# A two-layer decoder trunk: the MLPs' wide products in two halves of the tokens

## The chip, the cores and the metric

The kernel runs on one core of one Trainium2 chip. The metric is the device time of one execution in microseconds (us), shown as the median of several runs. The engines are TensorE (PE, matmuls; its weight loads are listed apart as PEld), VectorE (DVE), ScalarE (ACT), GpSimd (POOL) and SyncE (SP, which issues most DMAs). Each has its own queue of instructions, and they wait for one another by semaphores.

## The reference

Two layers, 512 tokens, 1024 features. Each layer is a mixer (layer 0: sliding-window attention beside a short convolution; layer 1: gated linear attention), an MLP, and a gated embedding of the layer. The MLP, cut to what matters here:

```python
D_MODEL, SEQ, D_FF = 1024, 512, 2816

def _conv_ffn(h, w_up, conv_w, conv_b, w_down):
    u = _causal_depthwise_conv(h @ w_up, conv_w) + conv_b      # width 3, over the tokens
    gate, up = jnp.split(u, 2, axis=-1)
    return (jax.nn.gelu(gate, approximate=False) * up) @ w_down

# in each layer i
x = x + mixer(rms_norm(x, mix_norm[i]))
x = x + _conv_ffn(_rms_norm(x, ffn_norm[i]), ffn_w_up[i], ffn_conv_w[i], ffn_conv_b[i], ffn_w_down[i])
x = x + _per_layer_embedding(x, p[i], ple_norm[i], ple_w_gate[i], ple_w_proj[i])
```

## The kernel before

*Numbers.* All is float32. An operand is split into a high part in the type that PE reads in one pass (float32r) and the rest, the low part; a product is then three matmuls, high by high, high by low and low by high (`mm3`, L162, lines 166 to 168). ACT makes the high part with a copy, DVE the low part with a subtraction: `split` (L100) for activations, `cut` (L129) for weights. The transposed activations `xT[m]` hold 128 features by 512 tokens; the operands of the MLP are `xg[k]`, eight pairs of 128 x 512. In a matmul here a block of 128 x 128 weights is loaded, and the tokens move past it: 512 columns in a plain product.

*Up-projection (`ffn`, L906).* A layer's 5632 columns are done in 11 groups of 256 gate columns and 256 value columns. The gate columns of a group go through a block scheme with seven products instead of eight (`seven`, L860): four weight blocks, two halves of the tokens, sums and differences of them as operands (`forms`). Each of the seven has 4 steps of three matmuls (lines 875 to 877), each over 256 tokens, one half. Their weights are cut by `cut_blocks` (L812) and `first_forms` (L834), which place the high parts 16 and the low parts 48 elements into their buffers (`BLOCKS`, L58). The two value columns of a group are plain products (`value`, L950): 8 blocks of rows with three matmuls of 512 columns. Their weights come from `column` (L947) with no offset. PE's order is written out by hand: `begin` (L962) puts six of a value column's eight blocks, the first block product, and the last two blocks; then the loop has a part of the seven products, four blocks of the other value column, a part, the other four blocks, the last part. So in every group four stretches of wide matmuls stand between four of narrow ones.

*What follows a group.* `taps` (L923) multiplies the results by the norm's factor R and runs the convolution over the tokens: on DVE line 926 (or 929 and 932) and two of line 935, on ACT line 933. R comes late: `end_norm` and `spread` make it within the first group of a layer. Line 1064 is the Gelu on ACT, and `place` (L970) multiplies gate and value. The order on DVE, ACT, POOL and SP is not written by hand in the MLPs: a scheduler lays it out from costs and priorities.

*Loads.* Two raw buffers hold a group's weights, 1 MB each (line 944, issued by SP). A buffer is free for the next group when its last cut is done; the last cut of the gate weights is the one in `seven`, of the block `od`.

*Down-projection (`down`, L1091).* The 22 blocks of 128 rows are in three parts, A (rows 8 to 13), B (0 to 7) and C (14 to 21), and the output in four units of 256 columns, two banks of the accumulator each. A `plan` lists chunks of three or four row blocks. A and B are plain everywhere; C goes through the seven products in four units of layer 0 and three of layer 1, where it stands between the steps of plain chunks, one row block at a time (`steps`, L1203). Within a chunk the row blocks are the outer loop and the two banks the inner one. When a unit is done DVE adds its banks to `xT` (line 1184), and `finish` makes the next stage's operands from them. The last stage, `ple1` (L1326), begins with weights that lines 1351 and 1352 cut.

Of the kernel before, what the change touches and what calls it, by code (L numbers as in the profile page):

```python
# [1 line left out]

# [16 lines left out]
P = 128  # L19
S = 512  # L20
D = 1024
NT = S // P
ND = D // P
# [32 lines left out]


BLOCKS = (16, 48)  # L58


class Kernel:
# [64 lines left out]
        t = self.wp.tile([P, 2048], F32, tag="raw", name=self.nm("raw"), bufs=2)  # L126
        return t[:, : na * nb].rearrange("p (a b) -> p a b", b=nb)

    def cut(self, rv, by):  # L129


        nc = self.nc
        na, nb = rv.shape[1:]
        parts = []
        n = 2 if na * nb > 1024 else 1
        for k in range(n):
            if by == "b":
                a, b = na, nb // n
                v = rv[:, :, k * b : (k + 1) * b]
            else:  # L140
                a, b = na // n, nb
                v = rv[:, k * a : (k + 1) * a, :]
            h, l = self.weight_tiles()
            hv = h[:, : a * b].rearrange("p (a b) -> p a b", b=b)
            lv = l[:, : a * b].rearrange("p (a b) -> p a b", b=b)
            nc.scalar.activation(hv, v, AF.Copy)  # L146
            nc.vector.tensor_tensor(lv, v, hv.bitcast(F32), ALU.subtract)  # L147
            parts.append((hv, lv))

        def get(i, c0, c1):  # L150
            if by == "b":
                b = nb // n
                k = c0 // b
                h, l = parts[k]
                return h[:, i, c0 - k * b : c1 - k * b], l[:, i, c0 - k * b : c1 - k * b]
            a = na // n
            h, l = parts[i // a]
            return h[:, i % a, c0:c1], l[:, i % a, c0:c1]

        return get  # L160
# [651 lines left out]
    def cut_blocks(self, src, wide=True):  # L812

        nc = self.nc
        if wide:
            h, l = self.weight_tiles(BLOCKS)
        else:
            h, l = (
                self.sp.tile([P, S + 64], F32R, tag="sq", name=self.nm("t2"), bufs=2)[:, o : o + S] for o in BLOCKS
            )  # L820
# [13 lines left out]
    def first_forms(self, ev, od, raw=None):  # L834
# [5 lines left out]
        else:  # L840
            h, l = self.weight_tiles(BLOCKS)
            h, l = (x.rearrange("p (j u n) -> p j u n", u=2, n=P) for x in (h, l))
# [63 lines left out]
    def ffn(self, i, project, next_gain):  # L906


        nc, a, tc = self.nc, self.a, self.tc
# [5 lines left out]
        with tc.tile_pool(name=f"ffn{i}", bufs=1) as fp:  # L915
            self.mlp = fp
            kept, acts, fours = [None] * NF, [None] * NF, []
# [27 lines left out]
                return out  # L945

            def column(raw, c):  # L947
                return self.cut(raw[:, :, c * P : (c + 1) * P], "b")

            def value(w, ps, k0, k1):  # L950
                for k in range(k0, k1):
                    self.mm3(ps, w(k, 0, P), xg[k], start=k == 0, stop=k == ND - 1)

            def prepare(d):

                rv, rg = loaded(d)
                w1 = column(rv, 1)
                ev, od = self.by_parity(rg)
                ws = self.seven_forms(ev, od, rg)
                return self.seven(od, ws, xg, self.forms), w1, column(rv, 0)  # L960

            def begin(d, steps, w):  # L962

                ps = self.pa()
                value(w, ps, 0, 6)
                next(steps)
                value(w, ps, 6, ND)
                return lambda y: taps(y[:, 1], ps, NF + 2 * d + 1)
# [61 lines left out]
            xg = self.xg  # L1030
# [60 lines left out]
    def down(self, i, acts, forms, both, work, finish):  # L1091
# [5 lines left out]
        rows = {"A": (8, 14), "B": (0, 8), "C": (14, 22)}  # L1097
# [15 lines left out]
        got, cuts, gens, pending = {}, {}, {}, []  # L1113

        def pend():
            while pending:
                pending.pop(0)()
# [4 lines left out]
        def load(key):  # L1122
            k0, k1 = rows[key[0]]
            u = int(key[1])
            raw = self.raw(k1 - k0, 2 * P)
            nc.sync.dma_start(raw, wd[:, k0:k1, cols(u)])
            got[key] = (raw, None)

        def load_inner(key):
            k0, k1 = rows[key[0]]  # L1130
            u = int(key[1])
            parts = []
            for q in range(2):
                t = both().rearrange("p a (b n) -> p (a b) n", n=2 * P)
                nc.sync.dma_start(t, wd[:, k0 + q : k1 : 2, cols(u)])
                parts.append(t)
            got[key] = (None, parts)

        def cut(t):
            u, name, k0, k1, _ = plan[t]  # L1140
            cuts[t] = self.cut(got[f"{name}{u}"][0][:, k0:k1], "a")
            if k1 == rows[name][1] - rows[name][0] and loads:
                load(loads.pop(0))

# [14 lines left out]
        def cut_done(u):  # L1159

            raw, _ = got[f"C{u}"]
            if raw is not None and loads:
                load(loads.pop(0))
            elif raw is None and inner:
                load_inner(inner.pop(0))

        todo = []
        for t, p in enumerate(plan):
            todo.append((1, lambda t=t: cut(t)))
            if p[4] is not None:  # L1170
                todo.append((1, lambda u=p[4]: first_forms(u)))
                todo.append((1, lambda u=p[4]: more_forms(u)))
        free = 3

        def pump(n):
            nonlocal free
            free += n
            while todo and todo[0][0] <= free:
                need, f = todo.pop(0)
                free -= need  # L1180
                f()

        def add(m, ps):
            nc.vector.tensor_tensor(self.xT[m], self.xT[m], ps, ALU.add)
# [5 lines left out]
        banks = {}  # L1190
        with tc.manual_schedule(engines={ET.PE}):
            with tc.high_priority(offset=300):
                for _ in range(2):
                    load(loads.pop(0))
                pump(0)
            for t, (u, name, k0, k1, s) in enumerate(plan):
                own = u not in banks
                if own:
                    banks[u] = [self.ps(), self.ps()]
                ends = t + 1 == len(plan) or plan[t + 1][0] != u  # L1200
                joined = i == 0 and u == 3

                def steps(lo, hi):  # L1203
                    for k in range(lo, hi):
                        for c in range(2):
                            self.mm3(
                                banks[u][c], cuts[t](k, c * P, (c + 1) * P), acts[rows[name][0] + k0 + k],
                                start=own and k == 0, stop=ends and k == k1 - k0 - 1, skip_group_check=joined,
                            )

                def settled(ends):
                    nonlocal next_unit
                    if ends:
                        for c in range(2):
                            add(2 * u + c, banks[u][c])
                        due[u] -= 1
                    while not block_left and next_unit < 4 and not due[next_unit]:
                        for m in (2 * next_unit, 2 * next_unit + 1):
                            finish(m)
                        next_unit += 1  # L1220

                if s is None:
                    steps(0, k1 - k0)
                    settled(ends)
                    pump(1)
                    pend()
                    if work:
                        work.pop(0)()
                        if not work:
                            load_inner(inner.pop(0))  # L1230
                else:
                    g = gens[s]
                    steps(0, 1)
                    next(g)
                    steps(1, 2)
                    next(g)
                    steps(2, 3)
                    next(g)
                    cut_done(s)
                    pump(1)  # L1240
                    steps(3, 4)
                    pump(1)
                    settled(ends)
                    X, Y, V = next(g)
                    pump(1)
                    x = self.xT[2 * s + 1].rearrange("p (u t) -> p u t", u=2)
                    nc.vector.tensor_tensor(x, x, V.unsqueeze(1).to_broadcast([P, 2, H]), ALU.add)
                    if i == 0 and s == 3:
                        banks[3] = [X, Y]
                    else:  # L1250
                        add(2 * s, X)
                        add(2 * s + 1, Y)
                    pend()
                    due[s] -= 1
                    block_left -= 1
                    settled(False)
# [720 lines left out]
```

## Time and profile before

| | us |
|---|---|
| median of 3 runs (1204.11 to 1204.66) | 1204.59 |
| the profiled execution | 1205.4 |
| its span, first to last instruction | 1203.6 |
| PE busy | 1196.3 |
| DVE busy | 968.4 |
| ACT busy | 665.5 |
| layer 0: first value column to the end of its MLP | 178 to 527 |
| layer 1: the same | 798 to 1144 |

Rows of the profile read like this. A group is "line, engine, operation, output<-inputs, shapes, xcount | busy us, mean ns of one | idle before it and what ended it". In the order of time a row begins with its start and its length in us. Matmuls overlap, so the length of one is not its cost. A row of busy time by stretch gives the stretch, its length, and for PE, PEld, DVE, ACT and POOL the busy time and the number of instructions, then PE's granted clock, the DMA share and GB/s. In the chain of waits a row is a start, a length and what the time went to. `four`, `a`, `b`, `uh`, `ul` are operands, `wh` and `wl` the high and low parts of weights, `ps` and `pa` accumulator banks, `zt` the taps' buffers.

### The profile page before, as it was taken

How to read it: one execution, taken by the hardware profiler on the slowest of the kernel's cores; microseconds unless marked ns; L12 is line 12 of the kernel's file. 1: busy time of each engine (PE TensorE's matmuls, PEld its weight loads, DVE VectorE, ACT ScalarE, POOL GpSimd, SP SyncE). 2: the span in 40 equal slices, each digit the busy share in tenths (PEclk: the TensorE clock that was granted, in tenths of full speed). 3: DMA queues.
4: the chain of work that ended last, by engine and by line, in shares of the span. 5: the costliest groups of instructions: out<-in, count | busy, mean ns of one | idle time of the engine just before them, and what ended most of it. 6: DMA issues, size and time to landing. Idle time of an engine off the chain costs nothing.

```text
span 1203.6 us, 17728 instructions
## 1 busy us (share of the span) xinstructions
PE 1196.3 (99%) x7018; PEld 1036.0 (86%) x7018; DVE 968.4 (80%) x1543; ACT 665.5 (55%) x1093; POOL 44.7 (4%) x64
## 2 busy tenths in 40 slices
PE   9999999999999999999999999999999999999998
PEld 8877789998899889888988988889998898888887
DVE  6786687899999987746679876678999998978595
ACT  7466565656465643534563654555565555645374
POOL 2600000000000000000100000000000000000000
PEclk9999999999999999999999999999999999999999
DMA  7232222424232332232322222323242423322601
GB/s 222 74 102 72 74 71 72 139 71 138 74 122 89 119 121 89 93 105 82 111 93 70 74 68 70 106 74 102 72 139 70 141 70 124 131 88 97 210 1 70
DMA packets 111127, 117.61 MB, mean 98 GB/s; under 512 B 2840, under 2 KB 106322, under 8 KB 111044
## 3 DMA queue, kind: packets, MB, share of 16 engines
q1 hardware_dynamic: 109680, 115.35, 29.4%
q8 instruction: 55, 0.90, 0.3%
q0 software_dynamic: 560, 0.42, 0.3%
q10 hardware_dynamic: 804, 0.70, 0.2%
q14 instruction: 28, 0.23, 0.1%
HBM read 114.37 MB, written 2.10 MB: 97 GB/s over the span
## 4 chain that ended last, share of the span: by engine, by line
PE 82%; DVE 12%; DMA 2%; ACT 2%; issue 1%; ACTq 0%; DVEq 0%
PE ps L166 14%; PE ps L167 14%; PE ps L168 14%; PE pa L167 5%; PE pa L166 5%; PE pa L168 5%; PE ps L875 4%; PE ps L877 4%; PE ps L876 4%; DVE zt L935 3%; DMA raw<-in_ffn_w_up_dram 2%; DVE wl L823 2%; PE pa L875 2%; PE pa L877 2%; PE pa L876 2%; DVE wl L147 1%
## 5 line engine op out<-in xcount | busy, mean ns | idle before, releaser
L146 ACT ACTIVATE wh<-raw 128x1024 fp32r<-128x1024 f32 (+4 forms) x154 | 152.3, 991 | 141.7 <-PE ps L167 101.3
L147 DVE TENSOR_TENSOR wl<-raw,wh 128x1024 fp32r<-128x1024 f32 (+4 forms) x154 | 175.1, 1138 | 52.9 <-ACT wh L146 52.3
L822 ACT ACTIVATE wh<-raw 128x1024 fp32r<-128x1024 f32 x78 | 82.8, 1061 | 120.6 <-DVE raw L847 65.4
L935 DVE SCALAR_TENSOR_TENSOR zt<-z,vfa,zt 128x510 f32<-128x510 f32 (+1 forms) x176 | 130.7, 744 | 11.7 <-ACT zt L933 11.2
L823 DVE TENSOR_TENSOR wl<-raw,wh 128x1024 fp32r<-128x1024 f32 x78 | 95.3, 1222 | 24.3 <-ACT wh L822 24.2
L933 ACT ACTIVATE zt<-z,vfb 128x512 f32<-128x512 f32 x88 | 71.0, 809 | 29.4 <-DVE four L986 12.8
L166 PE MATMUL ps<-b,wh 128*128 128x512 f32 x192 | 76.7, 399 | 0.0
L167 PE MATMUL ps<-b,wh 128*128 128x512 f32 x192 | 75.1, 391 | 0.0
L168 PE MATMUL ps<-b,wl 128*128 128x512 f32 x192 | 75.0, 391 | 0.0
L167 PE MATMUL pa<-b,wh 128*128 128x512 f32 x176 | 69.0, 392 | 0.0
L167 PE MATMUL pa<-a,wh 128*128 128x512 f32 x176 | 69.0, 392 | 0.0
L166 PE MATMUL pa<-a,wh 128*128 128x512 f32 x176 | 69.0, 392 | 0.0
L166 PE MATMUL pa<-b,wh 128*128 128x512 f32 x176 | 69.0, 392 | 0.0
L168 PE MATMUL pa<-a,wl 128*128 128x512 f32 x176 | 68.4, 389 | 0.0
L168 PE MATMUL pa<-b,wl 128*128 128x512 f32 x176 | 68.4, 389 | 0.0
L875 PE MATMUL ps<-four,wh 128*128 128x256 f32 x232 | 65.3, 282 | 0.7 <-ACT ps L896 0.7
L877 PE MATMUL ps<-four,wl 128*128 128x256 f32 x232 | 64.4, 278 | 0.0
L876 PE MATMUL ps<-four,wh 128*128 128x256 f32 x232 | 64.2, 277 | 0.0
L166 PE MATMUL ps<-a,wh 128*128 128x512 f32 x160 | 63.6, 398 | 0.0
L167 PE MATMUL ps<-a,wh 128*128 128x512 f32 x160 | 62.4, 390 | 0.0
L168 PE MATMUL ps<-a,wl 128*128 128x512 f32 x160 | 62.4, 390 | 0.0
L166 PE MATMUL ps<-uh,wh 128*128 128x512 f32 x128 | 50.3, 393 | 0.0
(472 smaller groups left out, 3495.6 us busy)
## 6 DMA issues: line engine op xcount, KB each, us to landing
raw<-in_ffn_w_up_dram SPq DMA_DIRECT2D x44, 1024.0 KB, 5.1
raw<-in_ffn_w_down_dram SPq DMA_DIRECT2D x13, 1024.0 KB, 4.8
raw<-in_hy_w_in_dram SPq DMA_DIRECT2D x8, 1024.0 KB, 5.2
raw<-in_gla_w_in_dram SPq DMA_DIRECT2D x8, 1024.0 KB, 5.1
raw<-in_ffn_w_down_dram SPq DMA_DIRECT2D x8, 768.0 KB, 4.2
raw<-in_ple_w_gate_dram SPq DMA_DIRECT2D x6, 1024.0 KB, 4.7
raw<-in_hy_w_out_dram SPq DMA_DIRECT2D x16, 256.0 KB, 4.0
raw<-in_gla_w_out_dram SPq DMA_DIRECT2D x4, 1024.0 KB, 4.8
```

The source lines that it names most:

```text
L146: nc.scalar.activation(hv, v, AF.Copy)
L147: nc.vector.tensor_tensor(lv, v, hv.bitcast(F32), ALU.subtract)
L166: mm(out, lh, rh, start=start, stop=False, **kw)
L167: mm(out, lh, rl, start=False, stop=False, **kw)
L168: mm(out, ll, rh, start=False, stop=stop, **kw)
L822: nc.scalar.activation(h, src, AF.Copy)
L823: nc.vector.tensor_tensor(l, src, h.bitcast(F32), ALU.subtract)
L875: mm(out, wh, xh, start=first and j == 0, stop=False, **kw)
L876: mm(out, wh, xl, start=False, stop=False, **kw)
L877: mm(out, wl, xh, start=False, stop=j == ND // 2 - 1, **kw)
L933: nc.scalar.activation(y, z, AF.Identity, scale=w2[:, f : f + 1], bias=bb[:, f : f + 1])
L935: nc.vector.scalar_tensor_tensor(out=y[:, tap:], in0=z[:, : S - tap], scalar=w[:, f : f + 1], in1=y[:, tap:], op0=ALU.mult, op1=ALU.add,)
```

## The change

Every wide product of both MLPs is done in two halves of the tokens, so that all matmuls there have 256 columns; and the weights of these products are placed in their buffers like the block products' weights, 16 and 48 elements in. In `value` all row blocks of a call are done for the first half, then for the second. In `steps` the bank becomes the outermost loop, then the half, then the row block. What is loaded, cut and summed is the same, and so are the loads; PE has 1776 more matmuls, each with its weight load.

```diff
+HALVES = (slice(0, S // 2), slice(S // 2, S))
...
-    def cut(self, rv, by):
+    def cut(self, rv, by, offs=(0, 0)):
...
-            h, l = self.weight_tiles()
+            h, l = self.weight_tiles(offs)
...
             def column(raw, c):
-                return self.cut(raw[:, :, c * P : (c + 1) * P], "b")
+                return self.cut(raw[:, :, c * P : (c + 1) * P], "b", BLOCKS)

             def value(w, ps, k0, k1):
-                for k in range(k0, k1):
-                    self.mm3(ps, w(k, 0, P), xg[k], start=k == 0, stop=k == ND - 1)
+                for c, k in itertools.product(HALVES, range(k0, k1)):
+                    self.mm3(
+                        ps[:, c], w(k, 0, P), [x[:, c] for x in xg[k]], start=c.start == 0 and k == 0,
+                        stop=k == ND - 1,
+                        skip_group_check=True,
+                    )
...
-            cuts[t] = self.cut(got[f"{name}{u}"][0][:, k0:k1], "a")
+            cuts[t] = self.cut(got[f"{name}{u}"][0][:, k0:k1], "a", BLOCKS)
...
                 def steps(lo, hi):
-                    for k in range(lo, hi):
-                        for c in range(2):
-                            self.mm3(
-                                banks[u][c], cuts[t](k, c * P, (c + 1) * P), acts[rows[name][0] + k0 + k],
-                                start=own and k == 0, stop=ends and k == k1 - k0 - 1, skip_group_check=joined,
-                            )
+                    for c, h, k in itertools.product(range(2), HALVES, range(lo, hi)):
+                        self.mm3(
+                            banks[u][c][:, h], cuts[t](k, c * P, (c + 1) * P),
+                            [x[:, h] for x in acts[rows[name][0] + k0 + k]],
+                            start=own and h.start == 0 and k == 0, stop=ends and k == k1 - k0 - 1,
+                            skip_group_check=True,
+                        )
```

More of the change, by code (lines that the diff above doesn't have):

```diff
@@ L1 @@
+import itertools
 from contextlib import ExitStack
@@ L1200, in down @@
                 ends = t + 1 == len(plan) or plan[t + 1][0] != u
-                joined = i == 0 and u == 3
                 def steps(lo, hi):
-                    for k in range(lo, hi):
-                        for c in range(2):
-                            self.mm3(
-                                banks[u][c], cuts[t](k, c * P, (c + 1) * P), acts[rows[name][0] + k0 + k],
-                                start=own and k == 0, stop=ends and k == k1 - k0 - 1, skip_group_check=joined,
-                            )
+                    for c, h, k in itertools.product(range(2), HALVES, range(lo, hi)):
[5 more added lines that the diff above has]
+                        )
                 def settled(ends):
```

## The prediction

> **What bounds the kernel now.** I read the page's busy shares and its chain of waits first, then the costliest groups, and then the order of time of TensorE (PE) inside the MLPs, where the change is.
>
> ```profile
> PE 1196.3 (99%) x7018; PEld 1036.0 (86%) x7018; DVE 968.4 (80%) x1543; ACT 665.5 (55%) x1093; POOL 44.7 (4%) x64
> PEclk9999999999999999999999999999999999999999
> PE 82%; DVE 12%; DMA 2%; ACT 2%; issue 1%; ACTq 0%; DVEq 0%
> ...
> L167 PE MATMUL pa<-a,wh 128*128 128x512 f32 x176 | 69.0, 392 | 0.0
> L875 PE MATMUL ps<-four,wh 128*128 128x256 f32 x232 | 65.3, 282 | 0.7 <-ACT ps L896 0.7
> ```
>
> PE is busy nearly always and at full clock; VectorE (DVE) carries 12% of the chain. A mean of 392 or 282 ns is the whole flight of one matmul; matmuls overlap, so what one costs is the distance from start to start:
>
> ```profile
> 362.88 0.28 PE L875 MATMUL ps<-four,wh 128*128 128x256 f32 x1
> ...
> 383.47 0.28 PE L875 MATMUL ps<-four,wh 128*128 128x256 f32 x1
> ...
> 417.70 0.39 PE L166 MATMUL ps<-four,wh 128*128 128x512 f32 x1
> ...
> 434.02 0.39 PE L166 MATMUL ps<-uh,wh 128*128 128x512 f32 x1
> ...
> 488.61 0.40 PE L166 MATMUL ps<-four,wh 128*128 128x512 f32 x1
> ...
> 489.99 0.28 PE L875 MATMUL pa<-a,wh 128*128 128x256 f32 x1
> 491.37 0.28 PE L875 MATMUL ps<-four,wh 128*128 128x256 f32 x1
> ...
> 494.09 0.40 PE L166 MATMUL ps<-four,wh 128*128 128x512 f32 x1
> ```
>
> From 417.70 to 434.02 stand 72 matmuls of 512 columns: 226.7 ns each. From 491.37 to 494.09 stand 24 of 256 columns: 113.3 ns, exactly half. Yet the first two rows are the same place in two groups of an up-projection, 20.59 us apart, and a group has 48 wide matmuls (two value columns, 8 x 3 each) and 84 narrow ones (seven block products of 4 x 3): 48 x 226.7 + 84 x 113.3 = 20.40 us. The missing 0.19 us lies where the width changes. After such a change the 12 narrow matmuls from 489.99 take 1.38 us where 12 steady ones take 1.36, and the six wide ones before them 1.38 instead of 1.36; products that follow one of their own width show nothing. A group has four stretches of each width, so eight changes: 0.19 / 8 = 24 ns per change.
>
> **The change, part by part.** (1) *Instructions.* Each wide matmul of the MLPs becomes two narrow ones with the same weights: 48 x 22 groups = 1056 in the value columns, and (56 + 64) row blocks x 2 x 3 = 720 in the down-projections, 1776 matmuls and as many weight loads more. At 2 x 113.3 against 226.7 ns that costs nothing. The rows are good to 0.01 us, so two narrow ones are 226.7 +- 0.85 ns, and the bound from both sides is 1776 x 0.85 = +-1.5 us; I take 0.
>
> A page of the Trainium skill speaks against it: "TensorE: Matmul & The Clock Gate", section "Back-to-back issue gap", gives a warm matmul N / 2.4 ns and about 2.5 ns more, whatever its width. By it a split would cost 2.5 ns and 1776 of them 4.4 us (an estimate from that page). The rows here do not agree: 512 columns are at 226.7, not near 216, and 256 at half of that.
>
> (2) *Width changes.* They vanish inside the MLPs. Up: 22 x 8; down: 7 blocked units x 8, as four products stand between wide steps. 232 x 24 ns = 5.5 us of PE time.
>
> (3) *What of this reaches the end.* Not all, since the first part of each up-projection is not bound by PE.
>
> ```profile
> 216.71 1.29 DVE L976 TENSOR_TENSOR u<-zt,zt 128x512 f32<-128x512 f32 x2 [2.47 <-ACT zt L1064]
> ...
> 236.97 1.29 DVE L976 TENSOR_TENSOR u<-zt,zt 128x512 f32<-128x512 f32 x2 [0.59 <-ACT zt L1064]
> ...
> 260.00:280.00 20.00, 20.00 (x129) 18.04 (x128) 19.94 (x30) 12.56 (x20) 0.00 (x0) 1.00 0.33 105
> ...
> 316.01 1.06 ACT zt L1064
> 317.07 0.28 ACT ps L896
> 317.40 0.39 PE ps L875
> ```
>
> In these rows (order of time of DVE; busy time by stretch, DVE third; chain of waits) DVE waits only for a Gelu that itself waits for DVE's taps, is busy for 19.94 of 20 us, and at 317.40 PE has to wait for it. What PE wins between DVE's first tap and 317 becomes a longer wait there. Only the four changes before R is there, which the taps need, come through: 0.1 us. From 317.4 to the end of layer 0's up-projection are 4.3 groups: up to 0.82 us. There a second loop runs, by the chain of layer 1:
>
> ```profile
> 957.20 5.05 DMA raw<-in_ffn_w_up_dram
> ...
> 962.34 1.07 ACT wh L822
> ...
> 977.54 5.46 DMA raw<-in_ffn_w_up_dram
> ...
> 998.30 6.39 DMA raw<-in_ffn_w_up_dram
> ...
> 1019.97 0.28 ACT ps L896
> ```
>
> The next weights land, are cut by ScalarE (ACT) and DVE, and the last cut frees the buffer for the next load: 20.34 us with a load of 5.05, 20.76 with one of 5.46. PE's new group would be 20.40. So the loop now runs beside PE. In layer 0 it left PE alone (no wait after 338 us); I keep 0.75. In layer 1 PE already waited for it (the copy at 1019.97 ends that wait), so I keep 0.3 and the same 0.1 at the start, between 0 and 1.0. Down: PE waits there for nothing but single copies; 4 x 8 x 24 ns = 0.77 us in layer 0 and 3 x 8 x 24 = 0.58 in layer 1, both kept.
>
> (4) *Order within the steps.* A down chunk now finishes its first bank at half time, and a chunk's later row blocks are read earlier. The first gives something once, at the end:
>
> ```profile
> 1143.77 1.37 DVE L1184 TENSOR_TENSOR xT<-xT,ps 128x512 f32<-128x512 f32 x2
> ...
> 1162.54 1.22 DVE L1352 TENSOR_TENSOR wl<-four,wh 128x1024 fp32r<-128x1024 f32 x1
> ...
> 1163.81 0.50 PE L167 MATMUL pa<-wl,four 128*128 128x512 f32 x1 [0.61 <-DVE wl L1352]
> ```
>
> From the last two sums on DVE is busy until the cut that PE waits 0.61 us for. One sum (0.68 us) can now go up to 2 us earlier (half a chunk of 18 x 226.7 ns), so I take 0.4 of the 0.61; bounds 0 and 0.61. The second can cost only if operands are late; the rows nearest to it are these:
>
> ```profile
> 351.91 0.28 PE L875 MATMUL pa<-four,wh 128*128 128x256 f32 x1
> ...
> 353.85 1.22 DVE L147 TENSOR_TENSOR wl<-raw,wh 128x1024 fp32r<-128x1024 f32 x1
> ...
> 414.55 1.22 DVE L106 TENSOR_TENSOR four<-four,four 128x1024 fp32r<-128x1024 f32 x1
> ```
>
> The third of the pair splits that the chunk at 417.70 needs ends at 415.8, 1.9 us ahead, so nothing waits; without that cover a chunk would lose up to 2 us. The scheduler also moves one DVE multiplication by R (L926) a place or two forward, ahead of the weight cut at 353.85; its value column is complete at 351.9, so it need not wait either. If it did, that cut, and behind it PE's next value column, would wait too.
>
> (5) *Weights placed at offsets 16 and 48.* The cuts do the same work, and block weights have these places already: 0 us.
>
> Sum: layer 0 0.1 + 0.75 + 0.77, layer 1 0.4 + 0.58, tail 0.4: 3.0 us. The profiled execution took 1205.4 us (span 1203.6 and 1.8 around it), 0.8 above the median of the three runs, so 1202.4 on its own time and **1201.6 us** on the median of 1204.59.
>
> **The rivals.** *All of it arrives* (DVE's early start moves along with PE): 5.5 + 0.4 gives 1198.7. Against it stands DVE's row of 19.94 of 20. *The loops take what is left of the up-projections*: only down, the starts and a little of the tail remain, 1.35 + 0.2, so 1203.0. For it: the slow loads of 5.46 and 6.39 us. *The change does not do what it says*: the 24 ns belong to another thing that also changes there, and stay: 1204.6; against it, products in a row of one width show none.
>
> *Slower: the narrow pitch does not hold for the converted products.* Such a pitch exists:
>
> ```profile
> 8.79 0.28 PE L168 MATMUL pa<-wh,a 128*128 128x256 f32 x1
> ...
> 9.51 0.28 PE L168 MATMUL pa<-wh,a 128*128 128x256 f32 x1
> ```
>
> Six matmuls of 256 columns in 0.72 us are 120 ns each, where weights move and tokens stand still. At that pitch a split costs 2 x 120 - 226.7 = 13.3 ns. Some 1300 splits lie on PE's path (1776 less 48 in each of the ten groups that DVE bounds): 17.3 us, less the 3.0 won, gives 1218.9. It decides the sign from 3.0 us / (2 x 1300) = 1.2 ns, a pitch of 114.5 ns. Against it: block products read the same halves of the tokens against weights at the same offsets at 113.3 ns. *A fixed cost per matmul*, at most the 0.85 ns that the rows leave open: 1300 x 0.85 = 1.1 us, 1202.7. By the 2.5 ns of that page of the Trainium skill it would be 3.3 us and 1204.9.
>
> **How the numbers follow.** Forecast 0.50 (own range 1200.4 to 1202.9), all arrives 0.12, loops take it 0.17, nothing changes 0.04, slow pitch 0.12, fixed cost 0.05. What a measurement can tell from no change is 0.2%, 2.4 us: faster means under 1202.2. The forecast lies there with 0.41 of its 0.50, and all of the second: faster 0.53. The same: 0.09 + 0.17 + 0.04 + 0.05 = 0.35. Slower: the slow pitch, 0.12. The range from 1198.9 to 1205.4 leaves out the slow pitch and the edges of the cases beside it.
>
> **What would show it.** Right: in an up-projection no change of pitch left and PE's group at 20.40 us after 317 us; PE's waits at the end of DVE's stretches longer by about 1 us per layer than now; in down, 113.3 ns throughout; the wait of 0.61 us before the last stage shorter. Wrong: a pitch above 114.5 ns in the converted matmuls; a rise of PE's waits by as much as the changes cost; or DVE idle time before L926 in its new place.

## The result

| | before | after |
|---|---|---|
| median (six runs each) | 1204.91 us | 1214.74 us |
| lowest to highest | 1204.11 to 1207.13 | 1213.73 to 1216.32 |
| the profiled execution, its span | 1205.4, 1203.6 | 1214.1, 1212.3 |

The changed kernel takes 1.0081 times as long, 95% interval 1.0068 to 1.0094: 9.8 us more, where 3.0 us less were forecast. It is slower, and outside the forecast's range. The granted clock is 1.00, as before.

### The profile after

The page of the changed kernel, busy times and the chain of waits:

```profile
PE 1200.9 (99%) x8794; PEld 1109.4 (92%) x8794; DVE 970.0 (80%) x1543; ACT 665.0 (55%) x1093; POOL 45.1 (4%) x64
PE 53%; DVE 33%; DMA 7%; ACT 4%; issue 3%; POOL 0%; ACTq 0%
```

DVE and ACT are as busy as before, to 2 us. But DVE now carries 33% of the chain of waits instead of 12%, and loads carry 7% instead of 2%. PE, which was held by its own work for 82% of the time, is so for 53%. So the round of the other engines and the loads has become longer.

The chain of waits of the changed kernel shows which one, in layer 0 (start, length, what; the way from one load of gate weights to the next):

```profile
339.23 5.49 DMA raw<-in_ffn_w_up_dram
344.80 1.07 ACT wh L825
345.90 1.23 DVE wl L826
...
360.13 5.30 DMA raw<-in_ffn_w_up_dram
...
380.86 6.76 DMA raw<-in_ffn_w_up_dram
```

This is the loop of the prediction: load, cut on ACT, DVE's chain, the last cut, which frees the buffer for the next load. It takes 20.9 us here. In the kernel before the load was issued at 337.75, DVE began at 344.04 and the next load was issued at 358.14 (rows below): 20.4 us. Of the 0.51 us, 0.38 lie between the issue and DVE's first cut (6.29 against 6.67), 0.13 in DVE's chain (14.10 against 14.23).

What has changed ahead of the load is the order on DVE. First the kernel before, the order of time of DVE and of SP (start, length, engine, line, operation; the value column's cut at 353.85, just ahead of the tap at 354.98, stands in the prediction):

```profile
337.75 0.37 SPq L944 DMA_DIRECT2D raw<-in_ffn_w_up_dram  x1
...
344.04 1.22 DVE L823 TENSOR_TENSOR wl<-raw,wh 128x1024 fp32r<-128x1024 f32 x1 [0.85 <-ACT wh L822]
...
354.98 0.74 DVE L935 SCALAR_TENSOR_TENSOR zt<-z,vfa,zt 128x511 f32<-128x511 f32 x1
...
355.09 0.37 SPq L944 DMA_DIRECT2D raw<-in_ffn_w_up_dram  x1
...
355.64 0.68 DVE L926 TENSOR_TENSOR z<-pa,R 128x512 f32<-128x512 f32 x1
...
356.90 1.22 DVE L823 TENSOR_TENSOR wl<-raw,wh 128x1024 fp32r<-128x1024 f32 x1
...
358.14 0.37 SPq L944 DMA_DIRECT2D raw<-in_ffn_w_up_dram  x1
```

and the same place of the changed kernel, whose lines 929, 938, 150, 826 and 947 are lines 926, 935, 147, 823 and 944 of the kernel before:

```profile
355.11 0.68 DVE L935 TENSOR_TENSOR z<-z,R 128x512 f32<-128x512 f32 x1
355.71 0.68 DVE L929 TENSOR_TENSOR z<-pa,R 128x512 f32<-128x512 f32 x1
356.31 1.21 DVE L150 TENSOR_TENSOR wl<-raw,wh 128x1024 fp32r<-128x1024 f32 x1
357.44 1.53 DVE L938 SCALAR_TENSOR_TENSOR zt<-z,vfa,zt 128x511 f32<-128x511 f32 x2
...
357.55 0.37 SPq L947 DMA_DIRECT2D raw<-in_ffn_w_up_dram  x1
...
358.89 1.22 DVE L826 TENSOR_TENSOR wl<-raw,wh 128x1024 fp32r<-128x1024 f32 x1
...
360.13 0.37 SPq L947 DMA_DIRECT2D raw<-in_ffn_w_up_dram  x1
```

The multiplication by R at 355.71 stands ahead of the value column's cut; before it stood behind it, at 355.64. It waits for nothing. But the cut frees the buffer of the value columns, and so their next load goes out 2.58 us ahead of the gate load instead of 3.05. The two transfers of 1 MB lie more over each other, and with that the wait for weights grows (that the overlap itself is the reason is not shown). The view of who waited for the loads of line 944 (before) and line 947 (after), as us and times:

```profile
  ACT wh L822: 20.6, 14
```

```profile
  ACT wh L825: 22.7, 14
  ACT wh L149: 7.7, 10
```

After the change the value columns' cuts (line 149) wait for their load too, ten times; before they never did.

To see where PE's time went, I took the distance from the start of each matmul to the next one, less the steady distance of its width (226.7 or 113.3 ns), in the up-projections of both layers, from 3 us ahead of the second group's gate load to the last Gelu. Distances up to 35 ns too long are summed as "width changes", longer ones as "waits" (some records may be missing, so a few tenths are uncertain):

| kernel | width changes, us | waits, us |
|---|---|---|
| before | 4.0 | 2.8 |
| after | 1.6 | 14.2 |

So most of the width changes went, as forecast, but the waits rose to five times what they were. The down-projections, by the same account, win 0.9 us of width changes and wait 1.3 us more.

### The profile page after: what moved, and what is told of

The parts are those of the page before. It is cut to its first block, busy times and chain, and to the rows that moved or that the text cites. A ratio compares the mean times of both kernels' runs of the same rounds, so it can differ in the third digit from the quotient of the medians.

```text
span 1212.3 us, 21274 instructions
## 1 busy us (share of the span) xinstructions
PE 1200.9 (99%) x8794; PEld 1109.4 (92%) x8794; DVE 970.0 (80%) x1543; ACT 665.0 (55%) x1093; POOL 45.1 (4%) x64
## 4 chain that ended last, share of the span: by engine, by line
PE 53%; DVE 33%; DMA 7%; ACT 4%; issue 3%; POOL 0%; ACTq 0%
PE ps L169 11%; PE ps L171 11%; PE ps L170 11%; DVE zt L938 7%; DMA raw<-in_ffn_w_up_dram 6%; DVE wl L826 6%; DVE wl L150 4%; DVE z L929 2%; PE ps L878 2%; PE ps L880 2%; PE ps L879 2%; ACT wh L825 1%; PE pa L170 1%; PE pa L171 1%; PE pa L169 1%
## 5 line engine op out<-in xcount | busy, mean ns | idle before, releaser
L171 PE MATMUL pa<-b,wl 128*128 128x256 f32 x352 | 98.0, 278 | 0.1
L171 PE MATMUL pa<-a,wl 128*128 128x256 f32 x352 | 97.8, 278 | 0.1
L169 PE MATMUL pa<-b,wh 128*128 128x256 f32 x352 | 97.3, 276 | 0.0
L170 PE MATMUL pa<-b,wh 128*128 128x256 f32 x352 | 97.3, 276 | 0.0
L169 PE MATMUL pa<-a,wh 128*128 128x256 f32 x352 | 97.3, 276 | 0.0
L170 PE MATMUL pa<-a,wh 128*128 128x256 f32 x352 | 97.3, 276 | 0.0
L169 PE MATMUL ps<-uh,wh 128*128 128x256 f32 x256 | 70.9, 277 | 0.1
L171 PE MATMUL ps<-uh,wl 128*128 128x256 f32 x256 | 70.7, 276 | 0.0
L170 PE MATMUL ps<-ul,wh 128*128 128x256 f32 x256 | 70.7, 276 | 0.0
L171 PEld LDWEIGHTS pa<-b,wl 128*128 128x128 f32 x352 | 66.1, 188 | 1.2 <-DVE wl L150 1.0
L171 PEld LDWEIGHTS pa<-a,wl 128*128 128x128 f32 x352 | 66.1, 188 | 0.7 <-DVE wl L150 0.5
L170 PEld LDWEIGHTS pa<-b,wh 128*128 128x128 f32 x352 | 66.1, 188 | 0.0
```

What stands on the lines that cost most here:

```text
L169: mm(out, lh, rh, start=start, stop=False, **kw)
L170: mm(out, lh, rl, start=False, stop=False, **kw)
L171: mm(out, ll, rh, start=False, stop=stop, **kw)
```

## The experiments

Three theories. **Theory 1**: the converted matmuls do what was forecast, and the scheduler's new order on DVE and ACT costs some 12 us. Of the 1511 DVE instructions that the program lists 256 stand in another place, of ACT's 1032 it is 134; SP's but for two loads, and POOL's, do not move. **Theory 2**: twice the matmuls and weight loads slow down loads or DVE whatever the order. **Theory 3**: the placement, or the down-projection, is to blame. Each kernel below was compared with the kernel before on the same chip.

### The order alone, the matmuls alone

To set the order apart from the matmuls, each instruction of an engine is queued behind the one that stood ahead of it in the other kernel. Both kernels issue the same instructions on DVE and ACT, so an order is a list of places in the traced program (`ORDER`, left out here):

```diff
+def in_order(tc):
+    traced = list(tc.nc.cur_bb.bb.instructions)
+    for engine, text in ORDER.items():
+        mine = [i for i in traced if i.engine == engine]
+        ...
+        for x, y in zip(order, order[1:]):
+            tc.add_manual_dep(mine[y], mine[x].name, dep(), reason="in_order")
...
     Kernel(ctx, tc, a, out).run()
+    in_order(tc)
```

> The changed kernel's matmuls and placement, with every DVE and ACT instruction queued in the order of the kernel before (nothing left out; two loads on SP keep the changed kernel's order). Theory 1 (the changed order on DVE and ACT, above all the multiplication by R ahead of the value column's cut, costs about 12 us and the narrow matmuls themselves give the 1 to 3 us forecast): 1201 to 1204 us, ratio 0.997 to 1.000, the loop of an up-projection back at 20.4 us per group. Theory 2 (narrow matmuls slow loads or DVE whatever the order): 1211 to 1216, loop 20.9. Between these: both, in the measured shares.

> The kernel before with its wide matmuls and no placement, with every DVE and ACT instruction queued in the order of the changed kernel. Theory 1: 1212 to 1218 us (the order's cost without the gain of the matmuls), loop of an up-projection 20.8 us per group or more. Theory 2: 1204 to 1206, loop 20.4.

| kernel | median | ratio to before | 95% |
|---|---|---|---|
| changed matmuls, order of before | 1205.79 us | 1.0006 | 0.9997 to 1.0015 |
| matmuls of before, order of after | 1212.53 us | 1.0058 | 1.0044 to 1.0072 |

The order costs 8.95 us with the changed matmuls (1214.74 - 1205.79) and 7.4 with those of the kernel before (1212.53 against 1205.13 in the same comparison). Theory 2 falls: the old matmuls lose as well when the order is the new one. But theory 1 is only half right. With the old order the forecast gain does not come either: 1205.8, not 1201 to 1204. This kernel cannot be told from the kernel before.

### One half of the change at a time

Only `value` in halves, then only `steps`, each with the weights placed for it and the order that the scheduler makes of it. The edit of the first, against the changed kernel (the second puts `column` and `value` back instead):

```diff
-            cuts[t] = self.cut(got[f"{name}{u}"][0][:, k0:k1], "a", BLOCKS)
+            cuts[t] = self.cut(got[f"{name}{u}"][0][:, k0:k1], "a")
...
-                    for c, h, k in itertools.product(range(2), HALVES, range(lo, hi)):
+                    for k in range(lo, hi):
+                        for c in range(2):
```

> Only the value products of the up-projections have 256 columns and placed weights; the down-projections are those of the kernel before. All of the loss was seen in the up-projections (layer 0's last Gelu 4.0 us later, layer 1's another 5.0 us). Theory 1: 1212 to 1216 us. Theory 3 (the placement of the down-projection's weights, or its order, is what costs): 1201 to 1205.

> Only the down-projections have 256 columns and placed weights; the value products are those of the kernel before. Theory 1: 1203 to 1206 us, the up-projections unchanged. Theory 3: 1211 to 1216.

Value alone: 1212.03 us, ratio 1.0061 (1.0047 to 1.0074). Down alone: 1204.69 us, 0.9998 (0.9989 to 1.0007). The loss comes with the value columns: with them alone the scheduler already gives DVE the changed kernel's order all through layer 0's up-projection. Theory 3 falls as far as the down-projection goes. The down-projection by itself, for which 1.35 us and the tail had been counted, gives nothing that can be measured.

### Twelve places on DVE

Most of the 256 places are in the first groups and at the layers' ends. In the steady groups DVE's order differs in one thing alone: six times in each layer the multiplication by R stands two places ahead, in front of the value column's cut and of one tap. This kernel has the order of the kernel before and these twelve moves:

```diff
-        "... 367 380 369 381 395 382 ..."
+        "... 367 380 395 369 381-382 ..."
```

These are places in `ORDER` for one of the twelve: 395 is the multiplication by R, 369 the cut, 381 a tap.

> The changed matmuls with the DVE and ACT order of the kernel before (1205.8 us), except that in six groups of each layer the multiplication by R of the value bank stands two places ahead, in front of the value column's cut, as in the changed kernel: 12 moves and nothing else. Theory 1a (these moves delay the load of the next value columns by 0.5 us, so that it lies more over the gate load, and the loop gets 0.3 to 0.5 us longer in each group): 1208.5 to 1211.5 us. Theory 1b (the loss of the order comes from the first groups of each layer and the ends): 1205 to 1207.

1211.23 us, ratio 1.0043 (1.0029 to 1.0057): the twelve moves cost 5.4 us of the 8.95. The chain of waits, first with the order of the kernel before, then with the twelve moves, at the same place:

```profile
337.55 5.25 DMA raw<-in_ffn_w_up_dram
342.88 1.07 ACT wh L825
343.97 1.23 DVE wl L826
...
358.08 5.02 DMA raw<-in_ffn_w_up_dram
```

```profile
339.75 5.56 DMA raw<-in_ffn_w_up_dram
345.39 1.07 ACT wh L825
346.49 1.23 DVE wl L826
...
360.73 5.20 DMA raw<-in_ffn_w_up_dram
```

The loop goes from 20.53 to 20.98 us: 0.32 later at DVE's first cut, 0.13 in DVE's chain. In ten groups of the two layers the value columns' load now goes out 2.58 us ahead of the gate load instead of 3.05. Over the last six groups of both layers the median from gate load to first cut on ACT is 5.22 us in the first kernel and 5.48 in the second; single groups scatter from 4.9 to 7 us in both. These 0.26 and the 0.13, twelve times, are 4.7 of the 5.4 us.

The undoing of the same moves in the changed kernel:

> The changed kernel with whole gate loads and its own order, but for the 12 moves, which are undone. By their price in the other direction (5.4 us): 1208.5 to 1210.5 us. If they cost only together with the order of the kernel before: 1213 to 1216.

1208.80 us, ratio 1.0032 (1.0019 to 1.0044): 5.9 us are back. The price agrees from both sides within the noise, and 3.0 us of the order remain (1208.80 - 1205.79). PE's account says where: from the second to the fifth group of both layers PE waits 1.1 us with the order of before and 4.4 us in this kernel.

The value columns' cuts wait for their load more often too after the moves (1.1 us, once, with the order of before; 6.3 us, eight times, with the twelve moves). But in the chains of waits every load of the up-projections is a gate load: nine with the order of before, eleven with the twelve moves, thirteen in the changed kernel. By these chains it is the gate load through which the moves reach the end.

### The loop made shorter

If the loop is what the moves lengthen, and what swallows the gain, both must change when the loop falls below PE's time. The first cut of a group needs only 128 of the 256 gate columns, so the gate load is issued as two transfers:

```diff
                 for raw, c0 in zip(out, (DFF + 256 * d, 256 * d)):
-                    nc.sync.dma_start(raw, wu[:, :, c0 : c0 + 256])
+                    if c0 >= DFF:
+                        nc.sync.dma_start(raw, wu[:, :, c0 : c0 + 256])
+                        continue
+                    for c in (0, P):
+                        nc.sync.dma_start(raw[:, :, c : c + P], wu[:, :, c0 + c : c0 + c + P])
```

It moves no instruction on DVE or ACT.

> The kernel before, with each load of gate columns issued as two transfers of 128 columns, so that the first cut can start on half of it; the order on DVE and ACT stays that of the kernel before. If the loop of load, ACT and DVE holds the up-projection, its period of 20.4 us loses up to 2.4 us until PE binds at about 20.1: 1202 to 1204 us, PE gaps in the groups below 0.3 us each. If PE alone binds the kernel before: 1204.5 to 1206. If 512-byte rows make the load slower: above 1206.

> The changed matmuls, DVE and ACT in the order of the kernel before, and the gate load in two. If the loop swallowed what the narrow matmuls give (gaps of PE in the up-projections 7.2 us against 2.8 in the kernel before), the gain shows once the loop is shorter: 1198 to 1201 us, 3 to 4 us under the kernel before with the same split load. If the narrow matmuls give nothing of their own: the same time as that kernel.

> The changed kernel in its own order, with the gate load in two. If the order costs only because it makes the loop longer, most of its 9 us go: 1199 to 1204 us. If the order costs by waits of its own: 1209 to 1213.

| gate load in two | median | ratio to before | 95% |
|---|---|---|---|
| kernel before | 1203.44 us | 0.9986 | 0.9977 to 0.9995 |
| changed matmuls, order of before | 1201.52 us | 0.9966 | 0.9954 to 0.9979 |
| changed kernel, own order | 1204.89 us | 0.9998 | 0.9989 to 1.0007 |

The second kernel came out 0.5 us above its expected range, the third 0.9 us. The view of the waiting for the gate loads, in the kernel with the changed matmuls and the order of before, first with whole loads, then with the load in two:

```profile
  ACT wh L825: 22.5, 13
```

```profile
  ACT wh L825: 1.5, 3
...
DMA to landing us min/median/max: 3.6/4.8/6.4
```

The waiting for them falls from 22.5 us to 1.5, and no load of the up-projections is left in the chain of waits. The loop no longer binds, and PE does; the order of time of PE, the same matmul in two groups, first with the matmuls of the kernel before, then with the changed ones:

```profile
357.95 0.28 PE L875 MATMUL ps<-four,wh 128*128 128x256 f32 x1
...
378.54 0.28 PE L875 MATMUL ps<-four,wh 128*128 128x256 f32 x1
```

```profile
357.76 0.28 PE L878 MATMUL ps<-four,wh 128*128 128x256 f32 x1
...
378.16 0.28 PE L878 MATMUL ps<-four,wh 128*128 128x256 f32 x1
```

20.59 us and 20.40 us for a group: exactly the two numbers of the forecast. (The 20.1 us at which the first expectation had PE bind was too low: its group of 20.59 binds there.) Now the changed matmuls win 1.9 us (1203.44 - 1201.52), less than the 3 to 4 expected, but most of the gain is no longer swallowed. And the order costs 3.4 us instead of 8.95 (1204.89 - 1201.52): it has costs beside the loop.

Two kernels part these 3.4 us, both from the kernel of 1201.52 us. The first adds the twelve moves, the second what the changed kernel reorders on DVE and ACT in the first five groups of each up-projection:

> The kernel with the changed matmuls, the order of the kernel before and the gate load in two (1201.5 us), plus the same 12 moves of the multiplication by R that cost 5.4 us with whole gate loads. Theory 1a (they cost through the loop of load, ACT and DVE alone, which the split load leaves below PE's time): 1201 to 1202.5 us. If they cost in another way (DVE's own time, a later weight cut): 1205 to 1207.

> The same kernel of 1201.5 us, plus what the changed kernel reorders on DVE and ACT in the first five groups of each up-projection, and nothing of what it reorders later. The changed kernel with split loads has 3.9 us of PE gaps in these groups where that kernel has 1.0. If this part of the order costs what is left beside the 12 moves: 1204 to 1205 us. If the ends of the layers do: 1201 to 1202.

With the twelve moves 1202.77 us (ratio 0.9982, 0.9973 to 0.9991), with the first groups 1203.62 (0.9987, 0.9978 to 0.9996). So the twelve moves cost 1.25 us here instead of 5.4, a little more than expected, and the first groups 2.1, a little less. Together that is 3.35 of the 3.4 us; each of the ratios is good to 0.1%, about 1 us, so that they meet so closely is luck. PE's account below agrees in size: 0.8 us more for the first, 2.1 for the second. The account, in the up-projections as above:

| kernel | width changes, us | waits, us |
|---|---|---|
| before | 4.0 | 2.8 |
| after | 1.6 | 14.2 |
| changed matmuls, order of before | 0.5 | 7.2 |
| the same with twelve moves | 1.3 | 11.7 |
| before, gate load in two | 3.9 | 0.5 |
| changed matmuls, order of before, gate load in two | 0.4 | 2.6 |
| the same with twelve moves | 0.3 | 3.5 |
| the same with the first groups' order | 0.6 | 4.5 |

Rows one and three show the missing gain: 3.5 us of width changes went, and 4.4 us of waits came. Row five shows the kernel before without its loop's waits. Rows five and six show what of the gain is left in the up-projections when the loop is short: 3.5 us less of width changes, 2.1 more of waits, a gain of 1.4. In the down-projections the same two kernels differ by 1.0 us less of width changes and 0.4 more of waits.

### The placement

> The same kernel of 1201.5 us, without the placement of the converted products' weights (both tiles from their start again, 256 columns kept). Forecast of step 5, and theories 1 and 2: 1201 to 1202 us, matmuls 113.3 ns apart as before. Theory 3 (the placement is what makes 256 columns run at 113.3 ns): slower, with a pitch above 113.3 ns and 1 us for each 0.28 ns of it.

```diff
-                return self.cut(raw[:, :, c * P : (c + 1) * P], "b", BLOCKS)
+                return self.cut(raw[:, :, c * P : (c + 1) * P], "b")
...
-            cuts[t] = self.cut(got[f"{name}{u}"][0][:, k0:k1], "a", BLOCKS)
+            cuts[t] = self.cut(got[f"{name}{u}"][0][:, k0:k1], "a")
```

1222.78 us, ratio 1.0148 (1.0135 to 1.0162): 21.3 us above the same kernel with the placement. In the order of time of PE, 33 converted matmuls of a value column, first with the placement, then without:

```profile
364.56 0.28 PE L169 MATMUL pa<-a,wh 128*128 128x256 f32 x1
...
368.30 0.28 PE L169 MATMUL pa<-a,wh 128*128 128x256 f32 x1
```

```profile
369.12 0.28 PE L169 MATMUL pa<-a,wh 128*128 128x256 f32 x1
...
373.08 0.28 PE L169 MATMUL pa<-a,wh 128*128 128x256 f32 x1
```

3.74 us against 3.96: 113.3 ns each with the weights 16 and 48 elements in, 120.0 ns with both parts at their buffers' start. 3552 converted matmuls at 6.7 ns are 23.8 us; 21.3 arrived. So theory 3 is wrong about the loss of the changed kernel, which has the placement, but the placement is what gives 256 columns their pitch of 113.3 ns here. The expectation drawn from step 5, that leaving the placement out changes nothing, missed.

## Why the prediction was wrong

**(1) Instructions: right.** The pitch is 113.3 ns in the converted products. A group with 48 splits takes 20.40 us, no more than 180 matmuls at 113.3 ns, so there is no fixed cost in it. By the 2.5 ns of the Trainium skill, "TensorE: Matmul & The Clock Gate", section "Back-to-back issue gap", the group would take 20.52, an estimate from that page. The section gives the 2.5 ns for an isolated matmul; in the stream here the measurement decides, and it says none.

**(2) Width changes: right.** 20.59 to 20.40 us per group, eight changes of 24 ns, once the loop is short.

**(3) What reaches the end: wrong in size.** The loop was seen and put "beside PE", with 0.85 us kept in layer 0's up-projection, 0.4 in layer 1's, and 1.35 in down. With the order of the kernel before nothing was kept: 1.0006 (0.9997 to 1.0015). A loop of 20.34 to 20.8 us and a PE group of 20.40 are not side by side: each load that lands late makes a wait that PE's longer group of 20.59 had in part covered, and the waits in the up-projections rose from 2.8 to 7.2 us. That is the rival "the loops take what is left", which had a chance of 0.17 and a time of 1203.0; even that was more than 2 us too good. With the loop shortened 1.9 us came, of the 3.0. By PE's account 1.4 of it is from the up-projections, where 1.25 had been forecast, and only some 0.6 from the down-projections, where "both kept" had counted 1.35: single waits there grew as the changes of width went.

**(4) Order within the steps: here is the step that failed.** "The scheduler also moves one DVE multiplication by R (L926) a place or two forward, ahead of the weight cut at 353.85; its value column is complete at 351.9, so it need not wait either." It does not wait, that was right. But it was costed at nothing for this alone. It runs for 0.68 us ahead of a cut that frees a buffer, whose load runs beside the load that the loop waits for. The prediction had this loop a step earlier, with its length for two different loads, and did not put the moved instruction on it. Such a move occurs twelve times, and together they cost 5.4 us, 0.45 each on average. The rest of the new order costs 3.0 us more and was not looked at. Most of it lies in the first groups of each layer (2.1 us, measured with the short loop; 3.3 us more of PE's waits there with whole loads); these had been written off as bound by DVE, where PE's gain gets lost, and that a change of order there can cost was left out. The smaller part of the step, a sum that goes earlier at the end, came with half its size. The wait of 0.61 us in the last stage became 0.42 (order of time of PE in the changed kernel):

```profile
1172.66 0.50 PE L170 MATMUL pa<-wl,four 128*128 128x512 f32 x1 [0.42 <-DVE wl L1359]
```

**(5) Placement: 0 us as a cost, right, but it was not the idle detail that the step made of it.** Without it the rival's pitch holds to the digit: 120 ns (that the rows at 8.79 us have it for the same reason was not tested). The price came out at 21.3 us, where 17.3 had been worked out for 1300 splits. The argument against this rival, that block products read weights at the same offsets at 113.3 ns, was the right one.

The last part of the prediction named "a rise of PE's waits by as much as the changes cost" as what would make it wrong. That happened, and then the order came on top. Its slower rival was a pitch; no rival was a moved instruction, though one such move stood in the text.

Not settled: why the scheduler lays out DVE and ACT in another way when only PE's instructions and two tiles' starts change, and whether the gate load lands later because it lies more over the value columns' load. The runs show the shift of the issue and the later landing together, and that the moves cost 1.25 us instead of 5.4 when the first half is enough to begin; a load without its neighbour was not tried. Nor was it looked at what makes the first groups' order cost 2.1 us.

## What to carry to other kernels

A scheduler may answer a change on one engine with a new order on the others: compare the orders first, and price each moved instruction by its length on the chain of whoever stands behind it (a buffer, its load, the loop), not by whether it has to wait. Where two loops are as close as here (20.3 to 20.8 us and 20.4), a gain in one may show only after the other is shortened: here the split load and the old order, which alone gave 1203.4 and 1205.8 us, together make the fastest kernel of this study, 1201.5 us, 0.9966 of the kernel before (0.9954 to 0.9979). Convert a product together with its weights' placement, which was worth 21.3 us here, and read the pitch of the converted rows before anything else.

## What the runs showed of the hardware

- A matmul of 256 columns of float32r starts every 113.3 ns or every 120.0 ns, and what decides here is where the two weight tiles start in their buffers: 16 and 48 elements in, or at the start (the two kernels differ in nothing else). The Trainium skill, "SBUF — State Buffer", section "Who interferes with whom", gives TensorE two read ports, one for the moving operand and one for weight loads, independent of each other. That gives no reason for the start of a weight tile to matter; here it cost 6.7 ns in each matmul. What conflicts, and which of the two starts does it, was not tested.
- Half a gate load does not land in half the time. Whole loads of 1 MB had a median of 5.1 us in the kernel before, the fastest 4.7. The transfers of 512 KB had a median of 4.8 us, the fastest 3.6; the median counts both halves of a load, the second issued right behind the first. The Trainium skill, "DMA: Bandwidth & Descriptors", section "Anatomy of one DMA — SWDGE (gpsimd) path", has a fixed part of about 2 us in each transfer on another path than this one. From the fastest of each, 1.1 us apart for half the bytes, a fixed part of 2.5 us follows, an estimate from these two figures and near that page's. The split helps since the first half is enough to begin.
